# Quarter sums on VectorE alone, and another order of output tiles, in a two-layer hybrid decoder step

## The chip, the cores and the metric

The kernel runs on one core of one Trainium2 chip. The metric is the device time of one execution in microseconds, given as the median of several runs. The engines are named as the profile names them: PE (TensorE), DVE (VectorE), ACT (ScalarE), POOL (GpSimd) and SP (SyncE, which issues the transfers).

## What is computed

One inference step through two decoder layers, for 1104 tokens (16 meta tokens, 1024 of a prompt, 8 x 8 sampled ones) of width 1024, all in float32:

```python
def trunk_layer(x, pos, lw, states, front_pad, chunk, attend):
    m, new_states = hybrid_mixer(rmsnorm(x, lw['g_pre_mix']), pos, lw, states, front_pad, chunk, attend)
    x = x + rmsnorm(m, lw['g_post_mix'])
    gate, up = jnp.split(rmsnorm(x, lw['g_pre_ffn']) @ lw['w_ffn_in'], 2, axis=-1)
    x = x + rmsnorm((jax.nn.silu(gate) * up) @ lw['w_ffn_out'], lw['g_post_ffn'])
    return x, new_states
```

`hybrid_mixer` runs three token mixers (gated delta rule, Mamba2 scan, sliding-window attention) on one input projection, concatenates their outputs to width 1024 and multiplies by `w_out`. The feed-forward part has a hidden width of 2816. The part around the change is the output projection `mixed @ w_out`, the two norms behind it, and the product with `w_ffn_in`.

## The kernel before

**Number format.** Every float32 matrix is split into a high and a low float16 half. One float32 product is three float16 matmuls (high-high, high-low, low-high; `mm3`, `mm3x`). The weights are split on the chip: ACT writes the high half, DVE the low half by one scalar_tensor_tensor (tile `wsp`).

**Stages of a layer.** Input projection and attention; the Mamba scan; the delta-rule heads; the output projection; the two norms and transposes; the feed-forward input product; the feed-forward output product. `dense` is the generator that issues the large matmuls and everything else is woven in between.

**Order of the work.** No order of instructions is written out by hand. `Plan` keeps an estimated clock for each engine (`RATE`, `HOP`); `P.run` picks, among generators with priorities, the one that is ready first, and the program is emitted in that order. A layer beneath it may still move instructions within an engine's queue. Each engine then works through its queue strictly in order.

**Output projection (in `dense`).** The nine token tiles (eight of 128 tokens and tile 8 of 80) are taken in the order `OUT_SEQ`. A tile is 48 matmuls of 512 columns; tiles 6, 7 and 8 (`part`) have seven eighths of the sum done earlier, stored in `od`, and only 6 matmuls left. The product leaves PSUM (tile `pd`, two buffers) by ACT, or by DVE for the three partial tiles. Then `out_post` runs for the tile, a chain over four engines: squares and their sum (ACT), multiplication by a gain (`m<-m,gpo`, in `post_norm`), the inverse root (two POOL instructions on 128x1, `rqy`), `xt<-m,rqy,xt` (DVE), squares again (ACT), `rqy` (POOL), `m<-xt,rqy,gpf` (DVE), eight transposes (PE, `ps_tr` and `ps_ch`), and the split into `xn` (ACT high, DVE low).

**Feed-forward input product.** It is computed by a Strassen-like scheme of seven half-size products in place of eight. The activations are cut into quarters: tokens of even and of odd tiles, and two halves of the inner dimension. `combos` forms the sums of quarters, piece by piece: piece q holds tiles 2q and 2q+1, all tokens in five pieces. A piece is some 13 element-wise operations of 128x512 (tiles `tm`, `st`, `xn`); `("S1", l, q)` and `("S3", l, q)` are its marks, which products 6 and 7 wait for. `load7` forms the sums of weight quarters (tile `raw`). The first four hidden tiles (`NPRE`) have products 1 and 2 done ahead, from the even tiles 0, 2, 4, 6, 8 alone. Each half-size product is 24 matmuls into two PSUM banks (256 and 296 columns); four pairs of banks go round. Products 5 and 7 end with sums of half-size products (`U<-U,hid` and `hid<-U,hid`).

**Who does the sums.** The sums in `combos`, `load7` and the gain in `post_norm` go through `tt`, which gives each to DVE or POOL, whichever the plan's clocks have free first. The sums behind products 5 and 7 are written for POOL:

```python
elif n == 5:
    for o, o0, on in b2:
        act(o, q[:, o0:o0 + on])
        G.tensor_tensor(ub[:, o0:o0 + on], ua[:, o0:o0 + on], o, op=ADD)
```

Of the kernel before, what the change touches and what calls it, by code (L numbers as in the profile page):

```python
# [29 lines left out]
HB = ((0, 512), (1696, 1184))  # L30
HS = 0.5 * DS * DS * XS
NPRE = 4
OUT_SEQ = (0, 6, 8, 2, 4, 7, 1, 3, 5)
NPT = 3
EPS = 1e-6
FSEQ = (1, 2, 5, 6, 3, 7, 4)
# [4 lines left out]
def tsz(i):  # L41
    return 128 if i < 8 else 80
# [74 lines left out]
class Plan:  # L117
# [114 lines left out]
    def mark(self, *keys):  # L232
        for key in keys:
            self.done[key] = self.last
# [51 lines left out]
def build(tc, A, depth=DEPTH):  # L286
    nc = tc.nc
    P = Plan()
    P.pin = tc.keep_in_program_order
    V, S, G, T, DQ = (P.engine(e, k) for e, k in ((nc.vector, "V"), (nc.scalar, "S"), (nc.gpsimd, "G"),  # L290
                                                 (nc.tensor, "T"), (nc.sync, "D")))
# [11 lines left out]
    def act(out, in_, func=AF.Copy, **k):  # L303
        S.activation(out=out, in_=in_, func=func, **k)
# [2 lines left out]
        V.scalar_tensor_tensor(out, a, s, b, op0=op0, op1=op1)  # L307

    def tt(out, a, b, op):

        n = 1
        for x in out.shape[1:]:
            n *= x
        t = {k: max(P.clk[k], P.clk["T"]) + P.RATE[k][0] * n for k in "VG"}
        (V if t["V"] <= t["G"] else G).tensor_tensor(out, a, b, op=op)

    def vts(out, a, s1, s2=None, op0=ALU.mult, op1=None):
        if op1 is None:
# [4 lines left out]
    MUL, ADD, SUB, MAX = ALU.mult, ALU.add, ALU.subtract, ALU.max  # L323
# [34 lines left out]
    def PS(tag):  # L358
        n = {"tr": 1, "inv": 2, "ch": 1, "o": 2}[tag]
        t = psm.tile([128, 512], F32, tag=tag, bufs=n, name="ps_" + tag)  # L360
        P.take(tag, n, t)
        return t
# [18 lines left out]
    def room(n):  # L381
        return lambda: live[0] + n <= NG

    def hold(n=1):
        live[0] += n
        assert live[0] <= NG, live[0]
# [166 lines left out]
    def drop(key):  # L553
        w, where = slab.pop(key)
        if where == "g":
            free()
        else:
            wfree[where] += 1
# [180 lines left out]
    def hid_new(L):  # L739
        L.hp.append(tuple(big([128, RW], F32, "hid") for _ in range(2)))  # L740
# [93 lines left out]
    def dense():  # L834
        for L in LY[:depth]:
# [73 lines left out]
            for hf in range(2):  # L909
                yield tuple(wo[hf * 4:hf * 4 + 4])  # L910
                for i in part:
# [4 lines left out]
                    for q in range(2):  # L916
                        a = abp.tile([128, 256], F32, tag="a", name="mo")
# [10 lines left out]
            mark(("gains", l))  # L928
            for i in OUT_SEQ:
                C = tsz(i)  # L930
# [6 lines left out]
                if not L.first:  # L937
# [3 lines left out]
                yield (tuple(("mix", l, h, i) for h in range(4)) + (("ssm", l, i), ("swa", l, i))  # L941
                       + tuple(wo if i == OUT_SEQ[0] else ()))
                for hf in range(2):
# [34 lines left out]
            def gate(b1, cn):  # L978
                a = abp.tile([128, 384], F32, tag="a", name="a")[:, :cn]
                act(a, b1, AF.Tanh, scale=DS * 0.5)  # L980
                stt(b1, a, 1.0, b1, ADD, MUL)
# [26 lines left out]
            for c in range(NF):  # L1008
                if c >= NPRE and c % 2 == 0:
                    yield room(2)  # L1010
                    hold(2)
                    hid_new(L)
                for n, (sl, o) in ((1, (0, 0)), (2, (0, 1)), (6, (1, 0)), (5, (1, 1)), (7, (2, 0)), (3, (2, 1)),
                                   (4, (3, 0)))[0 if c >= NPRE else 2:]:
                    yield (("wi", l, c, sl),) + tuple(({6: "S1", 7: "S3"}[n], l, q) for q in range(5) if n > 5)
                    w = slab[("wi", l, c, sl)][0][:, o]
                    p = [PS(t) if t != "d" else psd.tile([128, 512], F32, tag="d", name="pd") for t in
                         (("d", "d"), ("inv", "inv"), ("o", "o"), ("tr", "ch"))[turn % 4]]
                    turn += 1
                    yield from half(p, w, 0, 512, ops[n])  # L1020
                    if o or sl == 3:
                        drop(("wi", l, c, sl))
                    for k, (q, (c0, cn)) in enumerate(zip(p, CH)):
                        q = q[:, :cn]
                        b1, b2 = hid_out(L, c, 0, k)[0][0], hid_out(L, c, 1, k)
                        ua, ub = U[:, 0, c0:c0 + cn], U[:, 1, c0:c0 + cn]
                        if n == 1:
                            act(ua, q)
                        elif n == 2:
                            V.tensor_tensor(b1, q, ua, op=ADD)  # L1030
                            gate(b1, cn)
                        elif n == 6 and c < NPRE:
                            for o, o0, on in b2:
                                V.tensor_tensor(ua[:, o0:o0 + on], q[:, o0:o0 + on], o, op=ADD)
                        elif n == 6:
                            V.tensor_tensor(ua, q, ua, op=ADD)
                        elif n == 5:
                            for o, o0, on in b2:
                                act(o, q[:, o0:o0 + on])
                                G.tensor_tensor(ub[:, o0:o0 + on], ua[:, o0:o0 + on], o, op=ADD)  # L1040
                        elif n == 7:
                            V.tensor_tensor(ua, q, ua, op=ADD)
                            for o, o0, on in b2:
                                G.tensor_tensor(o, ua[:, o0:o0 + on], o, op=ADD)
                        elif n == 3:
                            V.tensor_tensor(ub, q, ub, op=ADD)
                            stt(b1, ub, HS, b1, MUL, MUL)
                        else:
                            V.tensor_tensor(ua, q, ua, op=ADD)
                            a = abp.tile([128, 384], F32, tag="a", name="a")[:, :cn]  # L1050
                            act(a, ua, AF.Tanh, scale=DS * 0.5)
                            stt(a, a, 1.0, ua, ADD, MUL)
                            for o, o0, on in b2:
                                stt(o, a[:, o0:o0 + on], HS, o, MUL, MUL)
                            if k:
                                mark(("hid", l, c))
                    yield NOW
# [11 lines left out]
            for n in FSEQ:  # L1069
                bk = [psd.tile([128, 512], F32, tag="d", name="pd") for _ in range(2)] + [PS("o") for _ in range(2)]  # L1070
                for g in ((0,), (1,), (2,), (3,), (4, 5)) if n != 4 else ((0,), (1,), (2,), (3, 4, 5)):
                    yield tuple((x, l, n, q) for x in ("w2", "S2") for q in g)
                    ks = range(2 * g[0], min(2 * g[-1] + 2, NF // 2))
                    for t in (0, 2, 1, 3, 4):
# [7 lines left out]
                        for k in ks:  # L1082
                            w, x = slab["w2", l, n, k // 2][0], L.S2[n, k // 2]
                            o = k % 2 * 512
# [1025 lines left out]
    it = iter(range(NT))  # L2110
# [24 lines left out]
    for L in LY[:depth]:  # L2135
        l = L.l
        mx_st = ExitStack()
        L.gp = pool("gp", 1, stack=mx_st)
        L.coll = L.gp.tile([128, 18, 27], F32, tag="coll", bufs=1, name="coll")
        mark(("gp", l))  # L2140
        sub = ExitStack()
        L.swp = pool("swa", 1, stack=sub)
        P.add(0, swa_in(L))
        P.add(0, swa_out(L))
        P.add(1, gates(L))
        P.run(("swaend", l), ("gates", l), *((("zt", l, i), "st") for i in range(NT)))
        P.pin = None
        sub.close()
        sub = ExitStack()
        L.ssp = pool("ssm", 1, stack=sub)  # L2150
        it = iter(range(NT))
        P.add(1, ssm_pre(L, it))
        P.add(1, ssm_pre(L, it))
        P.add(0, ssm_seq(L))
        P.run(("ssmend", l), (("hT", l), "st"))
        sub.close()
        sub = ExitStack()
        L.dnp = pool("dn", 2, stack=sub)
        it = iter([(h, b) for h in range(4) for b in QUADS])
        P.add(1, dn_inv(L, "0", it))  # L2160
        P.add(1, dn_inv(L, "1", it))
        P.add(1, dn_prep(L))
        P.add(0, dn_chain(L))
        P.run(*(x for h in range(4) for x in (("chain", l, h), (("S", l, h), "st"), (("Sb", l, h), "st"))))
        free(4)
        mark(("cso", l))
        dma(A["cso"][l], L.coll)
        sub.close()
        mx_st.close()
        sub = ExitStack()  # L2170
        w2p[0] = pool("w2", 3, stack=sub)
        wfree["w2"] = 3
        sst = ExitStack()
        L.stp = pool("st", 1, stack=sst)
        L.st = L.stp.tile([128, 3, 4, 2, HT], F16, name="st")
        it = iter((4, 3, 0, 1, 2))
        P.add(2, combos(L, it))
        P.add(2, combos(L, it))
        P.add(2, hid_sums(L))
        P.add(2, hid_tails(L))  # L2180
        mark(("ffn", l))
        P.run(("hids", l))
        sst.close()
        L.fp = pool("ffn", 1, stack=sub)
        mark(("fp", l))
        if not L.last:
            P.add(1, setup(LY[l + 1]))
        it = iter((0, 1, 2, 3, 8, 4, 5, 6, 7))
        P.add(4, ffn_post(L, it))
        P.add(4, ffn_post(L, it))  # L2190
        P.run(("dense", l), *(x for i in range(NT) for x in (("fp", l, i), (("x", l, i), "st"))))
        wfree["w2"] = 0
        free(2 if L.last else 3)
        sub.close()
# [88 lines left out]
```

## Time and profile before

| | |
|---|---|
| median of 3 runs (lowest, highest) | 2874.75 us (2872.89, 2879.48) |
| the profiled execution: its time, its span | 2877.86 us, 2876.0 us |
| mean granted TensorE clock | 0.979 |
| PE busy | 2721.0 us, 95%, 19518 matmuls |
| DVE busy | 1995.5 us, 69%, 3720 instructions |
| ACT busy | 1306.4 us, 45%, 3075 |
| POOL busy | 862.0 us, 30%, 1166 |

"Span" is from the first to the last instruction. "Busy" is the share in which the engine executes an instruction; an instruction that waits inside its execution for something another engine holds counts as busy. The granted clock is TensorE's, 1.0 being 2.4 GHz and 0.5 being 1.2 GHz. Nearly all instructions carry one line number (L216, the helper that records them), so the rows are told apart by the tiles that they write and read.

### The profile page before, as it was taken

The numbers are of one execution on the slowest core, as the hardware profiler recorded it, in microseconds if no ns is written. First come the engines' busy times: TensorE is split into PE (matmuls) and PEld (weight loads), VectorE is DVE, ScalarE is ACT, GpSimd is POOL, SyncE is SP. The second block draws the span as 40 slices with busy tenths as digits, with TensorE's granted clock in tenths as the row PEclk, the third lists the DMA queues.
The fourth block names the chain that finished last, engine by engine and source line by source line (L and its number), as shares of the span: only waits on it lengthen the run. The fifth ranks groups of instructions, "written<-read, shape, count | busy, mean of one in ns | idle before, by whom it ended". The sixth has DMA issues, their size and how long they took to land. (4 is left out here: it accounts for less than half of the span.)

```text
span 2876.0 us, 49982 instructions
## 1 busy us (share of the span) xinstructions
PE 2721.0 (95%) x19518; PEld 1895.5 (66%) x19518; DVE 1995.5 (69%) x3720; ACT 1306.4 (45%) x3075; POOL 862.0 (30%) x1166
## 2 busy tenths in 40 slices
PE   7999999997899999999999999999986999999998
PEld 4767677764578888744458676767634888887443
DVE  6467666656876776768876686666468777676778
ACT  5435465554433333433554455555544333333344
POOL 3205423304643333200260062233156333321002
PEclk9999999999999999999999999999998999999999
DMA  5011100134111111242340111001241111113324
GB/s 193 29 62 54 40 31 31 39 104 132 67 59 60 52 52 60 93 118 98 128 142 27 57 48 47 31 31 57 86 145 57 64 52 53 60 52 103 114 99 148
DMA packets 76270, 213.98 MB, mean 74 GB/s; under 512 B 13489, under 2 KB 24945, under 8 KB 76001
## 3 DMA queue, kind: packets, MB, share of 16 engines
q1 hardware_dynamic: 76032, 210.79, 22.6%
q8 instruction: 153, 2.51, 0.4%
q14 instruction: 85, 0.69, 0.1%
HBM read 179.68 MB, written 33.04 MB: 74 GB/s over the span
## 5 line engine op out<-in xcount | busy, mean ns | idle before, releaser
L216 PEld LDWEIGHTS <-wsp 128*128 128x128 f16 x10560 | 1031.6, 99 | 323.4 <-issue 30.8
L216 PE MATMUL pd<-xn,wsp 128*128 128x384 f16 (+3 forms) x4308 | 729.5, 312 | 1.7 <-ACT m L216 1.7
L216 DVE SCALAR_TENSOR_TENSOR wsp<-raw,wsp 128x512 f16<-128x512 f32 (+2 forms) x412 | 403.7, 989 | 177.5 <-ACT wsp L216 175.0
L216 ACT ACTIVATE wsp<-raw 128x512 f16<-128x512 f32 (+2 forms) x412 | 299.3, 738 | 376.6 <-DVE raw L216 116.1
L216 PEld LDWEIGHTS <-hsp 128*128 128x128 f16 x1848 | 181.0, 98 | 222.3 <-DVE hsp L216 3.7
L216 PE MATMUL pd<-wsp,mixed 128*128 128x512 f16 (+1 forms) x864 | 215.2, 385 | 22.6 <-DVE m L216 18.0
L216 PE MATMUL pd<-wsp,hsp 128*128 128x512 f16 x924 | 224.2, 381 | 3.4 <-DVE hsp L216 1.7
L216 PE MATMUL ps_o<-wsp,hsp 128*128 128x512 f16 x924 | 222.2, 379 | 0.1
L216 POOL TENSOR_SCALAR rqy<-ss 128x1 f32<-128x1 f32 (+1 forms) x72 | 61.4, 853 | 522.0 <-ACT jk L216 390.9
L216 DVE SCALAR_TENSOR_TENSOR u<-R,lp_cw,u 128x512 f32<-128x512 f32 x216 | 180.4, 870 | 11.3 <-ACT u L216 10.4
L216 POOL TENSOR_TENSOR raw<-raw 128x512 f32<-128x512 f32 x86 | 112.1, 1304 | 252.2 <-DVE raw L216 238.7
L216 POOL TENSOR_TENSOR U<-U,hid 128x256 f32<-128x256 f32 x132 | 93.6, 738 | 271.5 <-ACT hid L216 271.5
L216 ACT ACTIVATE hsp<-hid 128x512 f16<-128x512 f32 x154 | 89.9, 620 | 182.6 <-PE ps_o L216 161.9
L216 PE MATMUL pd<-wsp,xn 128*128 128x512 f16 (+3 forms) x864 | 157.6, 334 | 3.1 <-ACT wsp L216 1.9
L216 PEld LDWEIGHTS <-mixed 128*128 128x128 f16 (+1 forms) x864 | 84.3, 101 | 102.7 <-issue 31.1
L216 PE MATMUL ps_inv<-xn,wsp 128*128 128x296 f16 (+1 forms) x1080 | 148.0, 281 | 0.9 <-ACT xn L216 0.9
L216 PE MATMUL ps_o<-xn,wsp 128*128 128x296 f16 (+1 forms) x1044 | 147.9, 284 | 0.0
L216 DVE TENSOR_TENSOR hsp<-hid,hsp 128x512 f16<-128x512 f32 x154 | 101.3, 684 | 41.6 <-ACT hsp L216 41.4
L216 PEld LDWEIGHTS <-xn 128*128 128x128 f16 (+1 forms) x864 | 86.7, 102 | 51.5 <-issue 4.7
L216 PE MATMUL pd<-st,wsp 128*128 128x296 f16 (+1 forms) x768 | 100.3, 289 | 17.9 <-ACT hid L216 11.8
L216 PE MATMUL ps_ch<-xn,wsp 128*128 128x296 f16 x480 | 115.0, 289 | 0.0
L216 PE MATMUL ps_tr<-xn,wsp 128*128 128x256 f16 x480 | 114.3, 273 | 0.0
(497 smaller groups left out, 4896.7 us busy)
## 6 DMA issues: line engine op xcount, KB each, us to landing
raw<-wfi SPq DMA_DIRECT2D x96, 512.0 KB, 3.5
raw<-wfo SPq DMA_DIRECT2D x50, 512.0 KB, 3.8
raw<-wf SPq DMA_DIRECT2D x44, 512.0 KB, 3.3
xd<-xt SPq DMA_DIRECT2D x24, 512.0 KB, 2.8
xt<-xd SPq DMA_DIRECT2D x24, 512.0 KB, 5.1
rawg<-wfo SPq DMA_DIRECT2D x20, 512.0 KB, 4.3
xt<-x SPq DMA_DIRECT2D x16, 512.0 KB, 6.2
raw<-wo SPq DMA_DIRECT2D x16, 512.0 KB, 3.3
```

The lines of the kernel that those rows point to most:

```text
L216: r = f(*a, **kw)
```

## The change

`tt` always takes DVE, and the sums behind products 5 and 7 go through `tt`, so that every sum is on DVE. The output projection takes its tiles in the order 0, 2, 4, 6, 8, 1, 3, 7, 5, and `combos` takes its pieces in the order 4, 0, 1, 3, 2, which follows that.

```diff
-OUT_SEQ = (0, 6, 8, 2, 4, 7, 1, 3, 5)
+OUT_SEQ = (0, 2, 4, 6, 8, 1, 3, 7, 5)
...
     def tt(out, a, b, op):
-        n = 1
-        for x in out.shape[1:]:
-            n *= x
-        t = {k: max(P.clk[k], P.clk["T"]) + P.RATE[k][0] * n for k in "VG"}
-        (V if t["V"] <= t["G"] else G).tensor_tensor(out, a, b, op=op)
+        V.tensor_tensor(out, a, b, op=op)
...
                                 act(o, q[:, o0:o0 + on])
-                                G.tensor_tensor(ub[:, o0:o0 + on], ua[:, o0:o0 + on], o, op=ADD)
+                                tt(ub[:, o0:o0 + on], ua[:, o0:o0 + on], o, ADD)
...
                             for o, o0, on in b2:
-                                G.tensor_tensor(o, ua[:, o0:o0 + on], o, op=ADD)
+                                tt(o, ua[:, o0:o0 + on], o, ADD)
...
-        it = iter((4, 3, 0, 1, 2))
+        it = iter((4, 0, 1, 3, 2))
```

420 instructions leave POOL (1166 before, 746 after): 132 `U<-U,hid`, 132 `hid<-U,hid`, 86 `raw<-raw`, 64 of `combos`, 6 `m<-m,gpo`.

**DVE, first layer, from the first tile's gain on.** `m_7804` is tile 0; `m_7874` is the tile that is projected second (tile 6 before, tile 2 now); `m_7916` is tile 8. Before:

```order
L216 TENSOR_TENSOR m_7804<-m_7804,gpo 128x1024
L216 SCALAR_TENSOR_TENSOR m_7874<-pd,m_7874 128x512
L216 SCALAR_TENSOR_TENSOR wsp<-raw,wsp 128x1024 x2
L216 SCALAR_TENSOR_TENSOR xt<-m_7804,rqy,xt 128x1024
L216 SCALAR_TENSOR_TENSOR xt<-m_7874,rqy,xt 128x1024
L216 SCALAR_TENSOR_TENSOR m_7916<-pd,m_7916 80x512
L216 SCALAR_TENSOR_TENSOR m_7804<-xt,rqy,gpf 128x1024
```

Now:

```order
L216 TENSOR_TENSOR m_7804<-m_7804,gpo 128x1024
L216 SCALAR_TENSOR_TENSOR mixed<-g__7788,nwd,mixed 128x80
L216 SCALAR_TENSOR_TENSOR xt<-m_7804,rqy,xt 128x1024
L216 SCALAR_TENSOR_TENSOR wsp<-raw,wsp 128x1024 x2
L216 SCALAR_TENSOR_TENSOR m_7804<-xt,rqy,gpf 128x1024
L216 TENSOR_TENSOR xn<-ps_tr,xn 128x4x128
L216 TENSOR_TENSOR xn<-ps_ch,xn 128x4x128
L216 SCALAR_TENSOR_TENSOR wsp<-raw,wsp 128x1024
L216 TENSOR_TENSOR m_7874<-m_7874,gpo 128x1024
```

The evacuations of partial tiles (`m<-pd`), which stood among the first tile's chain, come later; the gain of the second tile, which was POOL's, is in DVE's queue.

**DVE, first layer, around the first `U` (the evacuation of product 6 of hidden tile 0).** Before:

```order
L216 TENSOR_TENSOR hid<-ps_inv,hid 128x40
L216 TENSOR_TENSOR st<-tm,st 128x4x128
L216 SCALAR_TENSOR_TENSOR hid<-a,hid 128x256
L216 SCALAR_TENSOR_TENSOR hid<-a,hid 128x296
L216 SCALAR_TENSOR_TENSOR wsp<-raw,wsp 128x512
L216 TENSOR_TENSOR U<-pd,hid 128x256 x2
```

Now:

```order
L216 TENSOR_TENSOR st<-tm,st 128x4x128
L216 TENSOR_TENSOR tm<-tm,xn 128x512
L216 SCALAR_TENSOR_TENSOR wsp<-raw,wsp 128x512
L216 TENSOR_TENSOR U<-pd,hid 128x256
L216 TENSOR_TENSOR xn<-tm,xn 128x4x128
L216 TENSOR_TENSOR U<-pd,hid 128x256
L216 TENSOR_TENSOR U<-pd,hid 128x40
L216 SCALAR_TENSOR_TENSOR wsp<-raw,wsp 128x512
L216 TENSOR_TENSOR raw<-raw 128x512
L216 TENSOR_TENSOR tm<-xn,tm 128x512
L216 TENSOR_TENSOR U<-U,hid 128x256
```

Before, DVE's share of the sums of quarters is done at this point; now four operations on the last piece stand behind it.

**One hidden tile in the middle of the feed-forward product.** POOL before:

```order
L216 TENSOR_TENSOR hid<-U,hid 128x256 x2
L216 TENSOR_TENSOR hid<-U,hid 128x40
L216 TENSOR_TENSOR raw<-raw 128x512 x2
L216 TENSOR_TENSOR U<-U,hid 128x256 x2
L216 TENSOR_TENSOR U<-U,hid 128x40
```

DVE now:

```order
L216 TENSOR_TENSOR raw<-raw 128x512
L216 SCALAR_TENSOR_TENSOR wsp<-raw,wsp 128x512
L216 TENSOR_TENSOR U<-U,hid 128x256 x2
L216 TENSOR_TENSOR U<-U,hid 128x40
L216 SCALAR_TENSOR_TENSOR wsp<-raw,wsp 128x512
L216 TENSOR_TENSOR raw<-raw 128x512 x2
L216 TENSOR_TENSOR U<-pd,U 128x256
L216 TENSOR_TENSOR U<-pd,U 128x296
L216 TENSOR_TENSOR hid<-U,hid 128x256 x2
L216 TENSOR_TENSOR hid<-U,hid 128x40
```

All of POOL's rows stand in DVE's queue, between the evacuations from PSUM.

## Rows read from the trace of the kernel before

**Rows 1.** The page, busy time of each engine and its share of the span.

```profile
PE 2721.0 (95%) x19518; PEld 1895.5 (66%) x19518; DVE 1995.5 (69%) x3720; ACT 1306.4 (45%) x3075; POOL 862.0 (30%) x1166
```

**Rows 2.** Windows: length, busy us of PE, PEld, DVE, ACT, POOL, clock, DMA.

```profile
671.00:805.00 134.00, 101.78 (x566) 60.25 (x566) 102.45 (x121) 59.96 (x119) 78.00 (x76) 0.87 0.30 99
2093.50:2228.00 134.50, 99.49 (x555) 58.48 (x555) 104.25 (x124) 60.27 (x119) 79.06 (x76) 0.89 0.30 99
...
900.00:950.00 50.00, 50.00 (x428) 41.63 (x426) 34.09 (x69) 18.08 (x41) 16.20 (x21) 1.00 0.18 55
```

**Rows 3.** Timeline of PE, first layer, around the output projection: start, duration, instruction, idle before.

```profile
682.23 1.01 PE L216 MATMUL pd<-wsp,mixed 128*128 128x512 f16 x2 [7.34 <-DVE m L216]
...
694.81 7.93 PE L216 MATMUL pd<-wsp,mixed 128*128 128x512 f16 x36
...
738.34 1.09 PE L216 MATMUL ps_tr<-c,m 128*128 128x128 f32 x4 [3.74 <-DVE m L216]
...
775.34 1.09 PE L216 MATMUL ps_tr<-c,m 128*128 128x128 f32 x4 [7.68 <-DVE m L216]
...
797.06 5.47 PE L216 MATMUL pd<-st,wsp 128*128 128x296 f16 x23 [4.14 <-ACT hid L216]
```

**Rows 4.** Timeline of DVE, the same stretch.

```profile
672.21 1.22 DVE L216 TENSOR_TENSOR m<-m,gpo 128x1024 f32<-128x1024 f32 x1
...
676.21 3.36 DVE L216 SCALAR_TENSOR_TENSOR xt<-m,rqy,xt 128x1024 f32<-128x1024 f32 x1
...
764.12 1.21 DVE L216 TENSOR_TENSOR m<-m,gpo 128x1024 f32<-128x1024 f32 x1
765.26 0.68 DVE L216 SCALAR_TENSOR_TENSOR wsp<-raw,wsp 128x512 f16<-128x512 f32 x1
765.86 1.27 DVE L216 SCALAR_TENSOR_TENSOR xt<-m,rqy,xt 128x1024 f32<-128x1024 f32 x1
767.06 0.68 DVE L216 TENSOR_TENSOR xn<-ps_tr,xn 128x512 f16<-128x512 f32 x1
...
769.46 0.41 DVE L216 TENSOR_TENSOR hid<-ps_o,hid 128x256 f32<-128x256 f32 x1
769.79 0.51 DVE L216 TENSOR_TENSOR hid<-ps_inv,hid 128x256 f32<-128x256 f32 x2
...
785.37 1.65 DVE L216 TENSOR_TENSOR tm<-tm,xn 128x512 f32<-128x512 f32 x1
...
805.16 0.85 DVE L216 TENSOR_TENSOR U<-pd,hid 128x256 f32<-128x256 f32 x3
```

**Rows 5.** Timeline of POOL, the same stretch.

```profile
675.29 3.21 POOL L216 TENSOR_TENSOR m<-m,gpo 128x1024 f32<-128x1024 f32 x1 [2.59 <-ACT xn L216]
...
731.60 1.15 POOL L216 TENSOR_TENSOR tm<-xn 128x512 f32<-128x512 f16 x1
...
784.85 1.61 POOL L216 TENSOR_TENSOR tm<-xn,tm 128x512 f32<-128x512 f16 x1
```

**Rows 6.** Groups of DVE, 671 to 805 us: count, busy us, mean ns, idle before.

```profile
L216 DVE SCALAR_TENSOR_TENSOR xt<-m,rqy,xt 128x1024 f32<-128x1024 f32 x8 | 13.2, 1651 | 3.9 <-POOL rqy L216 3.9
L216 DVE SCALAR_TENSOR_TENSOR m<-xt,rqy,gpf 128x1024 f32<-128x1024 f32 x8 | 11.1, 1391 | 5.1 <-POOL rqy L216 5.0
...
L216 DVE TENSOR_TENSOR tm<-tm,xn 128x512 f32<-128x512 f32 x10 | 8.7, 875 | 2.1 <-POOL tm L216 2.1
...
L216 DVE TENSOR_TENSOR xn<-ps_tr,xn 128x512 f16<-128x512 f32 x8 | 5.5, 686 | 4.6 <-ACT xn L216 4.6
```

**Rows 7.** Groups of DVE, then POOL, 850 to 1200 us (the feed-forward product).

```profile
L216 DVE SCALAR_TENSOR_TENSOR wsp<-raw,wsp 128x512 f16<-128x512 f32 x120 | 106.0, 895 | 61.7 <-ACT wsp L216 60.9
...
L216 POOL TENSOR_TENSOR raw<-raw 128x512 f32<-128x512 f32 x34 | 43.3, 1274 | 115.4 <-DVE raw L216 115.4
L216 POOL TENSOR_TENSOR hid<-U,hid 128x256 f32<-128x256 f32 x36 | 25.4, 726 | 15.2 <-DVE U L216 15.2
```

## The prediction

> **What bounds the kernel now.** I read the page first, for the shares: PE is busy 95% of the span, DVE 69%, POOL 30% [rows 1]. A kernel like that can gain only where PE stands still or runs at half clock, so the next view is the windows. In the middle of the feed-forward input product PE is busy 50.00 of 50 us at clock 1.00 [rows 2]: nothing is to be had there, whatever the sums cost. From the output projection to the first product that needs the sums of quarters it is different. In the first layer PE is busy 101.78 of 134 us, at a mean clock of 0.87, and the second layer repeats that within a few us (99.49 of 134.5) [rows 2]. These two stretches, some 268 of the 2876 us, are what the change can shorten.
>
> The timeline of PE says what it waits for there: 7.34 us for a DVE operation on `m` (a PSUM buffer that has not been emptied), 3.74 and 7.68 us for transposes whose tile is late, 4.14 us for an evacuation [rows 3]. Behind a long wait the next four transposes take 1.09 us, the half-clock level, while matmuls of 512 columns run at 7.93 / 36 = 0.22 us elsewhere [rows 3].
>
> So DVE is late. The timelines of DVE and POOL side by side show why. `xt<-m,rqy,xt` takes 3.36 us at 676.21 [rows 4], and 1.27 us at 765.86 [rows 4]; in the first case POOL was in a `m<-m,gpo` of 3.21 us that began at 675.29 and ended at 678.50 [rows 5]. A 128x512 sum takes 1.65 us on DVE at 785.37 [rows 4] while POOL runs sums of 1.61 us back to back [rows 5]; DVE's wsp operation of that width takes 0.68 [rows 4]. An operation that reads PSUM keeps its time in the same stretch: `xn<-ps_tr,xn` has a mean of 686 ns over eight [rows 6]. So DVE operations with both inputs in SBUF and POOL's sums take turns. The Trainium skill (SBUF — State Buffer, "Who interferes with whom") states this: a DVE instruction with two SBUF inputs and a POOL instruction that reads SBUF exclude each other, and one with a single SBUF input does not; the traces agree, by these numbers.
>
> **The change part by part.** *Sums of the transition.* I take DVE's queue from tile 0's gain (672.21) to the first `U` (805.16) [rows 4]: 133.0 us before. Own work is counted by the distance from one start to the next when nothing interferes: 1.14 us for a 1024-column tensor_tensor (764.12 to 765.26), 0.60 for a 512-column operation (765.26 to 765.86), 1.20 for a 1024-column scalar_tensor_tensor (765.86 to 767.06), 0.33 for 256 columns (769.46 to 769.79) [rows 4]. The queue before holds 22 x 1.20 + 6 x 1.14 + 64 x 0.60 = 71.6 us, and about 7.8 of narrower ones in proportion: 79.4. The window has DVE busy for 102.45 of 134 us [rows 2], so about 23 us are stretching by POOL and 31.5 us are idle.
>
> The same piece of the queue after the change holds 22 x 1.20 + 9 x 1.14 + 87 x 0.60 = 88.9, and 10 of narrower ones: 98.9 us. The moved sums add 19.5 us, and the 23 us of stretching fall away, since what is left for POOL there is `rqy`, 128x1. Busy time thus hardly changes; what changes is the idle time. Of the 31.5 us, waits for POOL sums (`tm`: 2.1 in the largest group [rows 6]) go; 3.9 and 5.0 us before `xt` and `m` are waits for `rqy` at the end of a chain [rows 6], and 4.6 us before `xn` for ACT [rows 6], and these stay in part, though a fuller queue has other work to put there. The bounds are 31.5 (none goes) and 11 (about a third, the chain waits alone). I take 18, nearer to the lower end, since the three chain rows just named make 13.5 and every sum that DVE now has itself removes a hop to POOL and back. 98.9 + 18 = 117, against 133: 16 us a layer.
>
> *Four sums behind the first `U`.* Now 4 x 0.60 = 2.4 us of the last piece's sums lie behind it. Against that, PE has more in hand: the bank of 256 columns needs only pieces 0 and 1, which the new order of `combos` takes early, so up to 48 matmuls, 48 x 50 / 428 = 5.6 us by [rows 2], can go ahead of the last piece. Bounds of the two together: a loss of 2.4 and a gain of 5.6; I take +1, as the planner has not placed PE's work by DVE's true queue.
>
> *Order of the tiles.* It removes no matmul: 254 of the output projection and 192 of the products done ahead stand between the same two points before and after. With 0, 2, 4 first, PE has 48 matmuls, 10.4 us at 0.217, for each tile behind which the chain of the tile before runs; with 6 and 8 second and third it had 6 each. The 7.34 us wait stood at that spot [rows 3]. I give this no sum of its own: DVE's queue is the longer one (PE's own matmuls at full clock are 254 x 0.217 + 192 x 0.117 + some 8 of transposes, 86 us), so what PE does not wait for early it waits for late. It is needed for the 18: DVE gets tiles sooner. The transfers for `xt` and `m` are issued in the new order on SP; their landings are not waited for in rows 3, and I cost the move at nothing, covered by those matmuls.
>
> *Feed-forward product.* 264 sums of half-size products and most of the 86 of weights move to DVE. Per 50 us DVE is busy 34.09 [rows 2]. Over 350 us POOL has 34 `raw` sums, 70 of 256 columns of the two kinds (36 in the second kind's row) and 36 of 40 columns [rows 7]; on DVE that is 34 x 0.60 + 70 x 0.33 + 36 x 0.11 = 47.5, or 6.8 per 50 us. Of the 120 `wsp` operations at 895 ns, 895 - 680 = 215 ns each, 25.8 us or 3.7 per 50, is stretching that goes [rows 7, 4]. DVE then has 37.2 of 50 us, and PE, with four pairs of banks, keeps its 50.00. Cost: nothing; cover: the 13 us that DVE has free. If the cover goes, it is the slower rival below. A transfer that lands late now holds DVE instead of POOL; the queued evacuations behind it are what PE would feel, after about three products (24 x 0.117 = 2.8 us each).
>
> **Sum.** 16 + 1 = 17 us a layer, 34 in all. The profiled execution took 2877.86 us (span 2876.0, the rest around it) and would take 2844; the median of the runs is 3.1 us lower, so 2874.75 - 34 = 2841.
>
> **Rivals.** *A deeper cut.* Idle falls to 11 and PE uses what it has in hand: 133 - 98.9 - 11 = 23, and up to 5: 28 a layer, 2819. For it: PE's own 86 us leave room, and less half-clock time follows fewer long waits. Against: the chain of one tile has two `rqy`, two ACT squares, and the last tile has little to hide behind.
>
> *The idle time stays.* All 31.5 us remain because the chains and not POOL's sums set the pace: 98.9 + 31.5 = 130.4, 2.6 a layer, 2870. For it: 13.5 us of chain waits in three rows [rows 6]. Against: it needs the 19.5 us of added work to fill none of the gaps.
>
> *Slower: DVE's queue as the bound.* If the long durations are DVE's own at that place and not POOL's doing, the moved work is simply added: 133 + 19.5 a layer, 2874.75 + 39 = 2914; it decides from the point where stretching plus idle lost is less than the 19.5 added. In the feed-forward product the same reading gives 34.1 + 6.8 = 40.9 busy plus 60.9 us per 350 of waits for ACT [rows 7], 8.7 per 50: 49.6 of 50, the brink. For it: DVE is already the later engine. Against: 3.36 and 1.27 us for one shape, and PSUM readers that never stretch. The Trainium skill (Perfetto Trace Analysis, "Optimizing Scalar/DVE Operations") speaks for this rival where it says that with DVE saturated, giving work to GPSIMD may make sense; the same paragraph warns that the shared port may make that useless, and rows 4 and 5 show the second case.
>
> **How the numbers follow.** Forecast (about 17 a layer) 0.62, the deeper cut 0.18, idle stays 0.13, slower 0.07. The range: 2820 from the deeper cut, 2867 from 4 us a layer; outside lie most of the last two cases. What a measurement can tell from no change is 0.2%, 5.7 us; the third case lies at that edge, so 0.05 of it counts as faster and 0.08 as the same: faster 0.85, same 0.08, slower 0.07.
>
> **What would show it right or wrong.** Right: from tile 0's gain to the first `U` DVE takes 112 to 122 us in both layers; its `xt` groups have a mean near 1280 ns and `wsp` 128x512 near 680; POOL has only 128x1 there; PE is busy 50.00 of 50 in the middle of the feed-forward product. Wrong: means as long as before without POOL sums; idle time of DVE before `xt`, `m` and `xn` as large as before; new waits of PE for `U` or `hid` between the products.

## The result, and the profile after

| | before | changed |
|---|---|---|
| median (lowest, highest), us | 2874.36 (2872.89, 2879.48) | 2838.52 (2836.68, 2840.47) |
| ratio, 95% interval | | 0.9872 (0.9855 to 0.9889) |
| span of the profiled execution, us | 2876.0 | 2838.4 |

The median before is now of four runs. The changed kernel is 35.8 us faster; 2841 was predicted, with 34 us gained. Of the 37.6 us between the two spans, 18.0 lie between the first gain of the first layer and that of the second (1422.58 us before, 2076.22 - 671.63 = 1404.59 now), and 19.0 behind the latter.

The page of the changed kernel, to be held against [rows 1]:

```profile
PE 2717.6 (96%) x19518; PEld 1891.5 (67%) x19518; DVE 2056.0 (72%) x4140; ACT 1308.0 (46%) x3075; POOL 492.6 (17%) x746
```

All 420 instructions have moved, yet DVE is busy only 60 us longer, while POOL is busy 369 us less. The windows of the changed kernel (columns as in [rows 2]): the stretch of the first layer from tile 0's gain to the first `U`, and two pieces from the middle of the feed-forward product.

```profile
671.00:789.00 118.00, 99.66 (x585) 58.52 (x584) 101.45 (x156) 60.80 (x118) 28.53 (x36) 0.94 0.34 111
...
900.00:950.00 50.00, 50.00 (x428) 41.66 (x426) 37.55 (x90) 18.41 (x44) 0.00 (x0) 1.00 0.16 54
1050.00:1100.00 50.00, 50.00 (x428) 41.63 (x427) 38.49 (x93) 16.59 (x38) 0.00 (x0) 1.00 0.20 63
```

The stretch holds 585 matmul records (566 before), and DVE is busy in it as long as before (101.45 us against 102.45), though it executes 156 instructions and not 121. Its length is what shrank: PE now loses 18.3 us there and not 32.2, and its granted clock has a mean of 0.94 instead of 0.87, between the levels of 2.4 and 1.2 GHz. In the feed-forward product DVE is busy 37.6 to 38.5 of 50 us, and PE keeps 50.00 of 50.

DVE's timeline, same stretch, answers to [rows 4]:

```profile
671.63 1.22 DVE L216 TENSOR_TENSOR m<-m,gpo 128x1024 f32<-128x1024 f32 x1 [0.27 <-ACT xn L216]
...
786.43 0.68 DVE L216 TENSOR_TENSOR tm<-xn,tm 128x512 f32<-128x512 f16 x1
...
788.84 0.41 DVE L216 TENSOR_TENSOR U<-pd,hid 128x256 f32<-128x256 f32 x1
...
790.67 0.53 DVE L216 TENSOR_TENSOR U<-pd,hid 128x256 f32<-128x256 f32 x2 [0.82 <-PE pd L216]
```

From gain to `U` it is 117.2 us; before it was 133.0. The groups of DVE from 671.63 to 790.67 us (to the second bank of that `U`; columns as in [rows 6]):

```profile
L216 DVE SCALAR_TENSOR_TENSOR m<-xt,rqy,gpf 128x1024 f32<-128x1024 f32 x8 | 10.2, 1280 | 4.2 <-POOL rqy L216 4.2
L216 DVE SCALAR_TENSOR_TENSOR xt<-m,rqy,xt 128x1024 f32<-128x1024 f32 x8 | 10.2, 1278 | 1.9 <-POOL rqy L216 1.9
L216 DVE TENSOR_TENSOR tm<-tm,xn 128x512 f32<-128x512 f32 x15 | 10.1, 681 | 0.0
...
L216 DVE SCALAR_TENSOR_TENSOR wsp<-raw,wsp 128x512 f16<-128x512 f32 x9 | 6.1, 680 | 0.0
L216 DVE TENSOR_TENSOR xn<-ps_tr,xn 128x512 f16<-128x512 f32 x8 | 5.5, 685 | 3.2 <-ACT xn L216 3.2
...
L216 DVE TENSOR_TENSOR raw<-raw 128x512 f32<-128x512 f32 x8 | 5.4, 680 | 0.0
```

`xt` has a mean of 1278 ns (1651 before), a `tm` sum 681 (875); the PSUM reader `xn<-ps_tr,xn` is where it was (685, 686). POOL has only `rqy` left there:

```profile
L216 POOL TENSOR_SCALAR rqy<-ss 128x1 f32<-128x1 f32 x16 | 12.6, 790 | 49.4 <-ACT xn L216 49.2
L216 POOL TENSOR_TENSOR rqy<-rqy,mhalf 128x1 f32<-128x1 f32 x16 | 12.4, 776 | 1.3
```

DVE's busy time between tile 0's gain and the first `U` changed in two ways that cancel. Its instructions before, each set against the median of its shape in the changed kernel, were too long by 19.9 us in sum (20.4 in the second layer); that stretching is gone, and the moved sums have put about the same back: 101.63 us busy before, 101.05 now. The gain is in the idle time, 31.3 us before and 16.2 now. Before, DVE waited 9.4 us for results of POOL's sums, all groups together (2.1 of it in [rows 6]); the other large groups, from 672.21 to 805.16 us:

```profile
L216 DVE TENSOR_TENSOR raw<-raw 128x512 f32<-128x512 f32 x4 | 5.7, 1426 | 1.2 <-POOL raw L216 1.2
...
L216 DVE TENSOR_TENSOR tm<-xn,tm 128x512 f32<-128x512 f16 x3 | 3.0, 998 | 2.2 <-POOL st L216 2.2
...
L216 DVE TENSOR_TENSOR tm<-tm,xn 128x160 f32<-128x160 f32 x3 | 1.0, 325 | 3.6 <-POOL tm L216 3.5
```

These waits are gone, and those for `rqy`, over all widths, fell from 12.4 to 7.1 us. The two make up nearly all of the some 15 us of idle time that went.

In the feed-forward product, 850 to 1200 us, `wsp` comes down from 895 ns [rows 7] to 686:

```profile
L216 DVE SCALAR_TENSOR_TENSOR wsp<-raw,wsp 128x512 f16<-128x512 f32 x116 | 79.6, 686 | 52.3 <-ACT wsp L216 52.3
L216 DVE TENSOR_TENSOR raw<-raw 128x512 f32<-128x512 f32 x66 | 45.3, 686 | 1.1
```

PE's timeline shows what is left. The early waits of [rows 3] have shrunk to two of about 1.5 us and some below 1; the long one now stands at the end, where product 3's first bank (`ps_tr<-st`) waits for a sum of quarters:

```profile
679.28 0.63 PE L216 MATMUL ps_tr<-c,m 128*128 128x128 f32 x4 [1.51 <-DVE m L216]
...
770.43 1.36 PE L216 MATMUL ps_o<-xn,wsp 128*128 128x256 f16 x11 [1.44 <-DVE xn L216]
...
776.39 0.37 PE L216 MATMUL ps_tr<-st,wsp 128*128 128x256 f16 x1 [4.59 <-ACT st L216]
777.53 2.51 PE L216 MATMUL ps_tr<-st,wsp 128*128 128x256 f16 x11 [0.77 <-DVE st L216]
```

Behind that wait 11 matmuls of 256 columns take 2.51 us, the half-clock level, where 11 of the same shape took 1.36 just before.

### The profile page after: what moved, and what is told of

The parts are those of the page before. It is cut to its first block, busy times and chain, and to the rows that moved or that the text cites. A ratio compares the mean times of both kernels' runs of the same rounds, so it can differ in the third digit from the quotient of the medians.

```text
span 2838.4 us, 49605 instructions
## 1 busy us (share of the span) xinstructions
PE 2717.6 (96%) x19518; PEld 1891.5 (67%) x19518; DVE 2056.0 (72%) x4140; ACT 1308.0 (46%) x3075; POOL 492.6 (17%) x746
## 3 DMA queue, kind: packets, MB, share of 16 engines
q8 instruction: 153, 2.51, 0.4%
## 5 line engine op out<-in xcount | busy, mean ns | idle before, releaser
L216 PE MATMUL pd<-xn,wsp 128*128 128x384 f16 (+3 forms) x4308 | 722.0, 313 | 0.5 <-ACT hid L216 0.4
L216 DVE SCALAR_TENSOR_TENSOR wsp<-raw,wsp 128x512 f16<-128x512 f32 (+2 forms) x412 | 342.6, 833 | 153.0 <-ACT wsp L216 151.9
L216 PE MATMUL ps_o<-xn,wsp 128*128 128x296 f16 (+1 forms) x1044 | 141.9, 283 | 5.0 <-DVE xn L216 3.9
L216 DVE TENSOR_TENSOR raw<-raw 128x512 f32<-128x512 f32 x176 | 119.7, 685 | 3.2 <-DMA raw<-wfi 0.9
L216 PE MATMUL ps_inv<-st,wsp 128*128 128x256 f16 (+1 forms) x816 | 105.3, 285 | 6.8 <-ACT st L216 3.5
L216 DVE TENSOR_TENSOR W<-ps_inv,c 128x512 f16<-128x512 f32 (+1 forms) x120 | 70.9, 595 | 47.0 <-PE ps_inv L216 46.1
```

Of the source, the lines that this page charges most:

```text
L216: r = f(*a, **kw)
```

## The experiments

### First set: the parts of the change by themselves

Theory A is that of the prediction: POOL's sums hold up DVE's operations, and the time is DVE's queue. Theory B, the rival: the gain comes from the orders, or from fewer hops between engines. The diffs are against the changed kernel where nothing else is said, and the name in brackets is the one by which other expectations call a run.

**All sums on VectorE, both orders as before** (s1_sums_only).

```diff
-OUT_SEQ = (0, 2, 4, 6, 8, 1, 3, 7, 5)
+OUT_SEQ = (0, 6, 8, 2, 4, 7, 1, 3, 5)
...
-        it = iter((4, 0, 1, 3, 2))
+        it = iter((4, 3, 0, 1, 2))
```

> All sums on VectorE, tiles and pieces in the old order. Theory A (GpSimd's sums held VectorE up; the order only feeds VectorE sooner): most of the gain is here, 2844 to 2858 us, about 20 to 30 of the 36 us; from tile 0's gain to the first U VectorE takes 119 to 125 us, its wsp operations of 512 columns have a mean near 680 ns. Rival B (the order of tiles, by which TensorE no longer meets two short tiles in a row, makes the gain): 2865 to 2875 us, and the wait of some 7 us behind the two partial tiles stays.

Measured: 2827.47 us (2825.81 to 2828.47), ratio 0.9840 (0.9824 to 0.9857). Both theories missed it: the sums alone gain 46 us, more than the whole change. Added to them, the orders cost 11 us (9 by the ratios). From tile 0's gain to the first `U` DVE takes 111.2 us, less than the 119 to 125 expected; its `wsp` of 512 columns have the mean that was expected, 681 ns.

**The orders alone** (s2_order_only), the planner dealing the sums to DVE and POOL as before. The diff is against the kernel before.

```diff
-OUT_SEQ = (0, 6, 8, 2, 4, 7, 1, 3, 5)
+OUT_SEQ = (0, 2, 4, 6, 8, 1, 3, 7, 5)
...
-        it = iter((4, 3, 0, 1, 2))
+        it = iter((4, 0, 1, 3, 2))
```

> New order of tiles and pieces, sums dealt between VectorE and GpSimd as before. Theory A: 2862 to 2876 us, at most 12 us of the gain; VectorE's operations with two SBUF inputs stay long (wsp of 512 columns near 900 ns). Rival B: 2840 to 2850 us.

Measured: 2871.12 us (2866.59 to 2875.19), ratio 0.9986 (0.9976 to 0.9996), as theory A had it. The groups of DVE, 671 to 790 us, are stretched, and more than the 900 ns that were expected (over the whole stretch, to 800.79 us, the mean of seven `wsp` is 1287 ns):

```profile
L216 DVE SCALAR_TENSOR_TENSOR wsp<-raw,wsp 128x512 f16<-128x512 f32 x5 | 7.4, 1492 | 0.0
...
L216 DVE TENSOR_TENSOR st<-tm,st 128x512 f16<-128x512 f32 x5 | 5.5, 1121 | 1.8 <-ACT st L216 1.7
```

So the orders gain some 3 us while POOL shares the sums and cost 9 to 11 when DVE has them all: the parts of the change do not add up.

**The sums behind products 5 and 7 back on POOL** (s3_products_pool), all else as changed.

```diff
-                                tt(ub[:, o0:o0 + on], ua[:, o0:o0 + on], o, ADD)
+                                G.tensor_tensor(ub[:, o0:o0 + on], ua[:, o0:o0 + on], o, op=ADD)
...
-                                tt(o, ua[:, o0:o0 + on], o, ADD)
+                                G.tensor_tensor(o, ua[:, o0:o0 + on], o, op=ADD)
```

> The changed kernel, with the sums behind products 5 and 7 given back to GpSimd (264 instructions). Theory A: no difference, 2836 to 2843 us, since TensorE is busy all the time in the feed-forward product and VectorE has room either way; wsp of 512 columns goes up to 720 to 850 ns there. Rival C (these sums gave part of the gain, by shorter waits in the product): 2846 us or more.

Measured: 2839.49 us (2837.48 to 2843.97), ratio 0.9883 (0.9868 to 0.9898): no difference from the changed kernel. The window and, from 850 to 1200 us, the group show POOL's work and the longer `wsp` coming back, and PE not noticing:

```profile
900.00:950.00 50.00, 50.00 (x428) 41.63 (x427) 34.47 (x74) 16.81 (x41) 9.98 (x16) 1.00 0.16 55
```

```profile
L216 DVE SCALAR_TENSOR_TENSOR wsp<-raw,wsp 128x512 f16<-128x512 f32 x112 | 82.2, 745 | 54.1 <-ACT wsp L216 53.3
```

So 264 of the 420 moved instructions bring nothing and cost nothing that these runs can tell; the gain is in the stretch of the transition.

**The old order of pieces** in the changed kernel (s4_old_pieces).

```diff
-        it = iter((4, 0, 1, 3, 2))
+        it = iter((4, 3, 0, 1, 2))
```

> The changed kernel with the pieces of the quarter sums in the old order 4, 3, 0, 1, 2, tiles in the new order. Theory A with the bank of 256 columns going ahead: that bank's first products need pieces 0 and 1, which now come after piece 3, so the 5.6 us of matmuls in hand are lost: 2841 to 2850 us. Rival D (the order of pieces follows the tiles and has no worth of its own): 2836 to 2841 us.

Measured: 2841.56 us (2841.02 to 2842.29), ratio 0.9888 (0.9873 to 0.9903). With the new order of tiles the new order of pieces gives 3 us; the two intervals of the ratio overlap, and the time lies where the two expectations meet, so this run does not decide between them. PE's timeline shows why no 5.6 us are lost: the last piece is 2 in both orders, and here too all the first banks of 256 columns, up to product 3's (`ps_tr`), go ahead of the first bank of 296 that needs it:

```profile
781.68 2.50 PE L216 MATMUL ps_tr<-st,wsp 128*128 128x256 f16 x11 [1.72 <-DVE st L216]
783.98 1.83 PE L216 MATMUL ps_inv<-st,wsp 128*128 128x296 f16 x12
```

### Second set: does a POOL sum hold DVE up, and which order costs the 11 us?

Two kernels (d1_pool_reads and d2_pool_writes) give POOL extra work beside the sums of quarters, whose result nobody uses. Each `put` in `combos` is followed by an addition of one column, and then:

```diff
+            for _ in range(4):
+                nc.gpsimd.tensor_tensor(DMY, DMY, DMY, op=ADD)
```

(`DMY` is 128x256), or, in the second kernel, by operations that only write:

```diff
+            for _ in range(8):
+                nc.gpsimd.memset(DMY, 0.0)
```

DVE's and PE's instructions and their order are those of the changed kernel.

> The changed kernel, and GpSimd does extra work beside the sums of quarters whose result nobody uses: four 128x256 sums in SBUF for each sum of quarters that is split. No instruction of VectorE is changed. Theory A (a GpSimd sum holds up VectorE's operations with two SBUF inputs): VectorE's 512-column sums and wsp operations rise from about 0.68 us to 0.9 us or more in the stretch, the stretch from the first gain to the first U grows by 10 to 28 us a layer, 2855 to 2895 in all. Theory B (before, only the hops between the engines and the shared queue cost time): as the changed kernel, 2834 to 2843.

> The same, but GpSimd's extra work only writes: eight fills of 128x256 in place of the four sums. Theory A (only reading from SBUF collides): as the changed kernel, 2834 to 2843, means of VectorE's operations as there. Rival (any GpSimd work holds VectorE up): as d1_pool_reads, 2855 to 2895. Theory B: 2834 to 2843 here too, but then d1_pool_reads as well.

Measured: the sums 2894.79 us (2894.36 to 2897.44), ratio 1.0073 (1.0058 to 1.0088); the fills 2847.72 (2843.34 to 2848.34), ratio 0.9904 (0.9889 to 0.9918). The groups of DVE from tile 0's gain to the second bank of the first `U`, with POOL's sums (668.41 to 814.38 us):

```profile
L216 DVE TENSOR_TENSOR tm<-tm,xn 128x512 f32<-128x512 f32 x15 | 13.9, 929 | 0.0
...
L216 DVE SCALAR_TENSOR_TENSOR m<-xt,rqy,gpf 128x1024 f32<-128x1024 f32 x8 | 10.3, 1282 | 6.8 <-POOL rqy L216 6.8
...
L216 DVE SCALAR_TENSOR_TENSOR wsp<-raw,wsp 128x512 f16<-128x512 f32 x9 | 9.3, 1037 | 0.0
...
L216 DVE TENSOR_TENSOR xn<-ps_tr,xn 128x512 f16<-128x512 f32 x8 | 5.5, 684 | 3.2 <-ACT xn L216 3.2
```

With fills (668.40 to 792.24 us):

```profile
L216 DVE SCALAR_TENSOR_TENSOR m<-xt,rqy,gpf 128x1024 f32<-128x1024 f32 x8 | 10.3, 1284 | 8.3 <-POOL rqy L216 8.3
...
L216 DVE TENSOR_TENSOR tm<-tm,xn 128x512 f32<-128x512 f32 x15 | 10.2, 686 | 0.0
...
L216 DVE SCALAR_TENSOR_TENSOR wsp<-raw,wsp 128x512 f16<-128x512 f32 x9 | 6.2, 684 | 0.0
```

And the two stretches as windows, first with sums, then with fills:

```profile
668.41:814.38 145.97, 104.77 (x589) 61.51 (x588) 125.19 (x156) 60.60 (x117) 95.66 (x127) 0.86 0.26 90
```

```profile
668.40:792.24 123.84, 101.97 (x593) 60.66 (x592) 102.37 (x157) 60.43 (x117) 75.05 (x157) 0.92 0.30 106
```

The same some 156 DVE instructions take 125.19 us beside POOL's sums and 102.37 beside its fills; the changed kernel has 102.06 between the same two points. A `tm` sum goes from 681 to 929 ns, `wsp` from 680 to 1037, and the PSUM reader stays at 684. The stretch is 26.9 us longer with sums than in the changed kernel (119.04), twice that is 54, and 56 was measured. Theory A holds, and B, by which both kernels would equal the changed one, falls as the only cause. What B named is real but smaller: beside the sums DVE is also idle 3.8 us longer (20.8 against 17.0), and beside the fills, below, 4.5 us. The Trainium skill (SBUF — State Buffer, "Who interferes with whom") says that an operation of GpSimd that only writes to SBUF does not contend with one of VectorE that has two inputs there; the traces agree, by 684 and 1037 ns for the same `wsp`.

The fills are not free all the same: 9 us, where A had at most 4. No group of DVE operations is longer by more than some 10 ns, but the waits for `rqy` before `m` grow from 4.2 to 8.3 us: POOL's queue is in order, and the two instructions of `rqy` now stand among fills. With 4.8 us a layer (123.84 against 119.04) this makes the 9.

**Old order of tiles, new order of pieces** (e1_new_pieces), all sums on VectorE: the fourth cell of the two orders. This diff and the next are against the kernel with all sums on VectorE and both old orders.

```diff
-        it = iter((4, 3, 0, 1, 2))
+        it = iter((4, 0, 1, 3, 2))
```

> All sums on VectorE, old order of tiles, new order of pieces: the fourth cell of the two orders. Theory A (with the sums on VectorE its queue is the bound, and the two orders count separately): the pieces give 3 us, as between s4_old_pieces (2841.6) and the changed kernel (2838.5), the tiles keep their 11: 2820 to 2829. Theory B (the orders only fit one another, tile 7 comes before tile 1 and so its piece should too): the mixed pair loses what s1_sums_only had gained, 2832 to 2845.

Measured: 2838.32 us (2835.11 to 2840.06), ratio 0.9871 (0.9854 to 0.9888). B's number: the orders do not count separately. But B's reason is not borne out: either new order alone loses 11 to 14 us, and both together, which fit one another just as the old ones do, lose 11.

**One partial tile early, the other behind a full tile** (e2_spread).

```diff
-OUT_SEQ = (0, 6, 8, 2, 4, 7, 1, 3, 5)
+OUT_SEQ = (0, 6, 2, 8, 4, 7, 1, 3, 5)
```

> All sums on VectorE, tiles in the order 0, 6, 2, 8, 4, 7, 1, 3, 5: one partial tile early, the second one behind a full tile. Theory A (what counts is how soon VectorE gets tiles): the second cheap tile comes 10 us later, so a part of the 11 us between s1_sums_only and the changed kernel is lost: 2828 to 2836. Theory B (what counts is TensorE, which in s1_sums_only waits some 6 us behind the two partial tiles for their banks): these waits shrink and the time falls below s1_sums_only, 2815 to 2825.

Measured: 2826.67 us (2823.35 to 2830.72), ratio 0.9834 (0.9818 to 0.9850): the same as with the old order of tiles, between what the two theories had. It speaks against A of this run: the second cheap tile came later, and nothing was lost.

### Third set: what stands in front of the sums

That run put the simple story (DVE must get tiles early) in doubt, so I counted what DVE executes between tile 0's gain and the first `U` (where the two banks of `U` are evacuated apart, to the second). The other operations there differ by seven at most; what differs more is how many splits (`wsp`) and sums (`raw`) of weights of 512 columns, work for products that come later, stand among them:

| all sums on DVE | `wsp` + `raw` ahead | stretch, us | ratio |
|---|---|---|---|
| new tiles, old pieces | 10 + 9 | 119.8 | 0.9888 |
| the change | 9 + 8 | 119.0 | 0.9872 |
| old tiles, new pieces | 8 + 8 | 120.7 | 0.9871 |
| old tiles, old pieces | 5 + 5 | 111.2 | 0.9840 |
| partial tiles apart | 3 + 4 | 107.7 | 0.9834 |

The second layer has the same counts in each of the five.

For the old orders the two rows stand as follows (671.16 to 782.34 us):

```profile
L216 DVE TENSOR_TENSOR raw<-raw 128x512 f32<-128x512 f32 x5 | 3.4, 683 | 0.4 <-DMA raw<-wfi 0.4
L216 DVE SCALAR_TENSOR_TENSOR wsp<-raw,wsp 128x512 f16<-128x512 f32 x5 | 3.4, 681 | 0.0
```

Two kernels test it, the changed one (f1_weights_later) and the one with the old orders (f2_old_orders_weights_later), each with one condition more in `load7`, which holds this work back:

```diff
-            yield lambda: split[0] == my and ("ffn", key[1]) in done and wfree["w2"] + wfree["w"] > 0
+            yield lambda: (split[0] == my and ("ffn", key[1]) in done and wfree["w2"] + wfree["w"] > 0
+                           and (key[2] == 0 and k == 1 or all(("S1", key[1], q) in done for q in range(5))))
```

> The changed kernel (its orders of tiles and pieces), with one condition more in load7: the splits and sums of weights for every slab behind the second of hidden tile 0 wait until S1 of all five pieces is done. VectorE then has 5 wsp and some 4 raw operations of 512 columns fewer ahead of the first U than the changed kernel (9 and 8 there; 5 and 5 in s1_sums_only). Theory W (the 11 us between the changed kernel and s1_sums_only are mostly such work that has slipped ahead of the sums of quarters in VectorE's queue): 9 x 0.60 = 5.4 us a layer, 2826 to 2832. Theory F (they are VectorE's idle time early, because it gets its second and third tile late): 2835 to 2842.

> s1_sums_only (all sums on VectorE, old orders) with the same condition. Theory W: only one wsp and one or two raw operations fewer stand ahead of the first U, 1 to 2 us a layer: 2822 to 2828, hardly below s1_sums_only. Theory F: no difference, 2825 to 2830.

Measured: the changed kernel with the condition 2827.77 us (2826.02 to 2830.62), ratio 0.9841 (0.9826 to 0.9856); the old orders with it 2825.41 (2823.62 to 2826.22), ratio 0.9830 (0.9813 to 0.9847). The first has 5 + 5 ahead of `U`, three `raw` and four `wsp` fewer (669.80 to 783.67 us):

```profile
L216 DVE TENSOR_TENSOR raw<-raw 128x512 f32<-128x512 f32 x5 | 3.4, 682 | 0.0
L216 DVE SCALAR_TENSOR_TENSOR wsp<-raw,wsp 128x512 f16<-128x512 f32 x5 | 3.4, 681 | 0.0
```

These 7 x 0.60 = 4.2 us, of the 5.2 by which the stretch shrank (113.87 against 119.04), give back nearly all of the 11 us, without a change to the orders: by the ratios all (0.9841, and 0.9840 with the old orders), by the medians 44.1 us are gained on the kernel before as it ran beside this one, 35.8 by the changed kernel, 46.5 by the one with the old orders. The second has 4 + 4 ahead, and its time lies in what both theories expected of it; it could not tell them apart, the first does. The windows show that the early feeding does not matter. The changed kernel:

```profile
671.00:700.00 29.00, 25.58 (x124) 12.10 (x123) 18.61 (x21) 13.88 (x24) 8.34 (x12) 1.00 0.62 188
...
775.00:800.00 25.00, 18.80 (x110) 12.55 (x110) 24.18 (x48) 10.32 (x19) 0.00 (x0) 0.66 0.20 64
```

Changed kernel with the condition:

```profile
671.00:700.00 29.00, 25.44 (x123) 11.99 (x121) 19.00 (x22) 13.35 (x23) 8.09 (x13) 1.00 0.62 194
...
775.00:800.00 25.00, 22.71 (x175) 17.81 (x176) 24.59 (x58) 9.37 (x19) 0.00 (x0) 0.90 0.16 53
```

Old orders, all sums on DVE:

```profile
671.00:700.00 29.00, 21.83 (x98) 10.79 (x99) 23.65 (x34) 14.45 (x25) 8.08 (x13) 0.82 0.53 174
...
775.00:800.00 25.00, 23.28 (x191) 18.58 (x192) 25.00 (x59) 10.08 (x22) 0.00 (x0) 1.00 0.25 85
```

In the first 29 us DVE is busy 19.00 us in the second and 23.65 in the third, and their times are equal; with 18.61 us the changed kernel starts like the second. The difference is at the end: from 775 to 800 us PE has 110 matmul records at a mean clock of 0.66 in the changed kernel, 175 at 0.90 with the condition, 191 at 1.00 with the old orders. Theory F falls and W holds, with its size a little under the measured one. W does not reach further down: with 4 + 4 (old orders and the condition) and 3 + 4 (partial tiles apart) the stretch is 2 and 3.5 us shorter than with the old orders' 5 + 5, but the ratios, 0.9830 and 0.9834, do not differ from 0.9840 clear of noise. Why was not tried. A price shows too: held back, the weights are late in the changed kernel with the condition, where PE waits for a split, and 2.64 us more for another at 776.70:

```profile
771.29 2.31 PE L216 MATMUL ps_o<-xn,wsp 128*128 128x256 f16 x10 [4.26 <-DVE wsp L216]
```

So the condition is not the best one possible; it still beats the changed kernel, as do the old orders with or without it. Why the planner lets more weight work ahead in the new orders was not tried; it orders by its own estimated clocks.

## Why the prediction was right, step by step

- **The bound.** Right. PE gained nothing in the feed-forward product (50.00 of 50 both times) and 14 us in the first layer's stretch.
- **DVE stretched by POOL's sums.** Right, and now shown by cause: extra POOL sums bring the long durations back, fills do not. The size, 23 us, was a remainder; instruction by instruction it is 19.9.
- **117 us from gain to `U`.** Measured 117.2 in the first layer, and 116.6 in the second (2076.22 to 2192.82). The parts fit as well: 98.9 of own work and 18 idle were forecast; DVE is busy 101.05 us of the 117.21, idle 16.2. That the sum met 117 to 0.2 us is luck in part: one term is 2 us over and the other 2 under. The 18 was an estimate between bounds; that the waits for POOL's sums go and those for `rqy` and ACT stay in part is what happened.
- **Four sums behind the first `U`, +1.** The rest of the layer gave 18.0 - 15.7 = 2.3 us, within the -2.4 to +5.6 given, but no run separates this term from the rest. The 48 matmuls do go ahead, and they do so with the old order of pieces too, so that order had less to give than the reason for the +5.6 assumes. The second bank's `U` waits 0.82 us for PE, so the sums that stand behind the first bank do cost a little there.
- **Feed-forward product, nothing.** Right: 37.2 of 50 us were forecast for DVE, 37.6 and 38.5 measured, and with 264 of its sums moved back the time was the same within noise (2839.5 against 2838.5).
- **Order of the tiles: the step that failed.** It had no sum of its own and was called "needed for the 18: DVE gets tiles sooner". The idle time falls as far with the old orders (111.18 - 95.98 = 15.2 us), DVE gets its tiles later with the new ones (18.61 us busy between 671 and 700 us, 23.65 with the old), and the new orders cost 9 to 11 us: 46 us could be had from the sums alone. What I left out is what else the plan puts into DVE's queue. I counted the new queue as it stands, so the 17 splits and sums of weights ahead of `U` were in my 98.9 us and the total came out; but I took them for part of the price and not for something that the order of pieces and tiles had put there. By the same count for the old orders the forecast for the sums alone would have been lower than that for the whole change.
- **The rivals.** The deeper cut (2819) is what the sums alone (2827) come nearer to, by less work in the queue and not, as it had it, by less idle time. The idle time did not stay, and DVE's queue did not become a slower bound.

## What to carry to other kernels

Before work is split between DVE and POOL, compare one shape's duration on DVE with POOL busy and idle. If operations with both inputs in SBUF get longer, as here, set what DVE loses by that, and by waiting for POOL's results, against what it would have to do itself: here the first two were about 20 and 15 us in the first layer's transition, the last about 19. When an engine's in-order queue is the bound of a stretch, count what stands in it ahead of the instruction that the next stage waits for, and hold back whatever later stages need. Two edits that arrive together should be timed apart: here a gain of 46 us hid a loss of some 10.

## What the runs showed of the hardware

I had not expected the price of a POOL sum to be so much alike in two quite different mixtures: 72 sums of 128x256, in the row below from 668 to 813 us (and 18 additions of one column), added 23 us to DVE's busy time; before, 54.3 us of POOL's sums (78.00 us busy [rows 2], less the 23.7 that `rqy` took there) made DVE's instructions 19.9 us longer, by the count in the section on the result.

```profile
L804 POOL TENSOR_TENSOR dmy<-dmy 128x256 f32<-128x256 f32 x72 | 63.2, 877 | 5.6
```

So DVE lost 0.37 us for each microsecond of POOL's sums here (23.1 / 63.2), and as much before (19.9 / 54.3). And a POOL queue filled with writes (but for 18 or so reads of one column) slows nothing on DVE by more than some 10 ns an operation, yet still delays what DVE waits for from POOL, by 4.4 us in the first layer.
